# RoPE and scores of all position pairs: the first batch of q and k loaded in whole tiles of 2 MB

## The chip, the cores and the metric

The kernel runs on one core of a Trainium2 chip. The time is device time in microseconds (us). For the kernel before, five executions took 799.1 to 802.11 us, with a median of 801.0 us. One execution was profiled; it took 801.33 us.

The core's engines run side by side, each with its own list of instructions in a fixed order, and wait for one another by semaphores: PE (matrix multiply, with PEld for its weight loads), DVE (elementwise), ACT (elementwise and copies), POOL (unused here but for constants), and SP, which in this kernel only issues DMA transfers. DMA transfers move data between the main memory (HBM) and the on-chip memory (SBUF) on 16 DMA engines. SP's transfers go through one queue (q1), ACT's through another (q10).

## The reference

q and k have shape (16, 512, 16, 64): batch, position, head, dimension. Each is rotated position by position with cos and sin of shape (512, 32), and then the scores are taken for each batch and head (the index letters are those of the reference):

```
q1, q2 = q[..., :32], q[..., 32:]
q_rot = concat([q1*cos - q2*sin, q1*sin + q2*cos])     # k_rot likewise
scores = einsum('bshd,bthd->bsht', q_rot, k_rot)        # (16, 512, 16, 512)
```

So s and t are two positions of the same batch and h is a head: for every batch and head, all 512 x 512 position pairs. All is float32. The inputs are 67 MB, the output 268 MB.

## The kernel before

A batch's 512 positions are put on 128 partitions with C = 4 positions each (position = 4p + c), so that a whole batch of q or of k is one tile of 128 partitions x 16 KB: each partition's 16 KB is one contiguous run in HBM. Work goes in *steps* n = 0 to 63, four (c = 0 to 3) for each batch. For a step, DVE rotates 128 positions of all heads in place (`rope`: a product with `ss_t`, which holds sin and -sin, a product with cos, and an add; lines 146, 147, 151), PE transposes the result 128 columns at a time (`transposed`, L173) and ACT or DVE copies it back over its source (L174). `scores` (L181) then multiplies two heads at a time, and ACT copies the result from PSUM into a staging buffer (L188). When a step's 16 heads are done, SP stores 4 MB (L79).

The order of everything is written out by hand (`manual_schedule`): the order of the statements is the order on each engine. A transfer that stands behind another on SP is issued behind it.

Batch 0 is done differently, so that output can begin before all of it is rotated. Its q and k lie in `early`, the last third of the staging area, which is not yet needed for output. They are worked on in *units*: G = 4 heads of all four positions c, since the scores of a head need all 512 positions of k. `load_units` loads k and q of heads 0 to 3 (512 KB each, in runs of 4 x 64 x 4 B = 1 KB), then k and q of heads 4 to 15 (1.5 MB each, in runs of 3 KB). Behind these SP requests k and q of batch 1, 2 MB each in runs of 16 KB (`load`, L104).

The tables cos and sin, 64 KB each, are requested on ACT's queue (L203) ahead of all. ACT makes `ss_t` from sin (L210, L211). Then come the rope and the transposes of k unit 0 and q unit 0, and a loop over eight pairs of heads (`p` in `range(HP)`, L218): two pairs for each c, with a store of 1 MB (four heads, L222) after every second pair. In this loop stand the rope and transposes of k units 1 and 2 (`run(dve[:2])`, `tr_act`), k of batch 2 is requested after the second store (p = 3) and q of batch 2 after the fourth (p = 7), both L224. The next loop (`for i in range(C)`, L232) does heads 4 to 15 of batch 0, four stages of 3 MB (L251), while DVE goes on to batch 1; its first stage goes to a part of the staging area of its own, its second to where the first three 1 MB stores are read from, so that ACT waits there until these have landed. k of batch 3 is requested after the second of these stores and q of batch 3 after the fourth.

From step 4 on (L258) the staging area is used as three buffers of 4 MB, and k and q have three tiles each. ACT waits before it writes into a buffer whose store has not landed.

Of the kernel before, what the change touches and what calls it, by code (L numbers as in the profile page):

```python
# [10 lines left out]
def kernel(  # L11
# [8 lines left out]
    nc = tc.nc  # L20
    fp32 = mybir.dt.float32
# [3 lines left out]
    B, S, H, D = q.shape  # L25
    HD = D // 2
    P = 128
    C = S // P
    HP = H // 2
    NST = B * C  # L30
    G = H // C
# [3 lines left out]
    in_pool = ctx.enter_context(tc.tile_pool(name="in", bufs=2))  # L35
# [6 lines left out]
    dram = {  # L42
        "q": q.rearrange("b (p c) h d -> b p c h d", c=C),
        "k": k.rearrange("b (p c) h d -> b p c h d", c=C),
    }
# [20 lines left out]
    early = stage_t[:, 3 * RW :]  # L66
# [3 lines left out]
    def stage(i):  # L70
        at = (3 * RW, 0, W)[(i - C) % 3]
        return stage_t[:, at : at + W].rearrange("p (h t) -> p h t", t=S)

    def store(i, st):
        b, c = divmod(i, C)
        if i == NST - 1:
            last(o_v[b, :, c], st)
        else:
            nc.sync.dma_start(o_v[b, :, c], st)  # L79


    units = {}
    used = [0]

    def load_units(which, head, heads):
        n = C * heads * D
        t = early[:, used[0] : used[0] + n].rearrange("p (c e) -> p c e", c=C)
        used[0] += n
        src = dram[which][0, :, :, head : head + heads, :]
        nc.sync.dma_start(t.rearrange("p c (h d) -> p c h d", d=D), src)  # L90
        if which == "q" and head > 0:
            units["r"] = t
        for h in range(0, heads, G):
            units[which, (head + h) // G] = t[:, :, D * h : D * (h + G)]

    tiles = {}
    def load(which, b):

        if b >= B:
            return  # L100
        t = in_pool.tile([P, C, H * D], fp32, tag=which + "_in", bufs=3, name=which + "_sb")
        for c in range(C):
            tiles[which, C * b + c] = t, c
        nc.sync.dma_start(t.rearrange("p c (h d) -> p c h d", h=H), dram[which][b])  # L104

    def slot(which, n):
        if which == "r":
            return units["r"][:, n]
        t, c = tiles[which, n]
        return t[:, c]  # L110

    def unit(which, n):
        return which != "r" and n < C

    def rope(which, n):

        part = part_pool.tile([P, H * D], fp32, tag="part", name="part")
        if unit(which, n):  # L120
            x = units[which, n]
            cs = cos_t.unsqueeze(2).to_broadcast((P, C, 2 * G, HD))
            ss = ss_v.unsqueeze(2).to_broadcast((P, C, G, D))
            sv, k1, k2 = "p c (g j) -> p c g j", {"j": HD}, {"j": D}
            pv = part.rearrange("p (c g j) -> p c g j", c=C, j=D)
            x5 = x.rearrange("p c (h x j) -> p c h x j", x=2, j=HD)
            p5 = part.rearrange("p (c h x j) -> p c h x j", c=C, x=2, j=HD)
            adds = [(x5[:, :, :, y], p5[:, :, :, 1 - y]) for y in range(2)]
        else:
            x = slot(which, n)  # L130
            heads = x.shape[-1] // D
            part = part[:, : heads * D]
            c = n % C
            cs = cos_t[:, c].unsqueeze(1).to_broadcast((P, 2 * heads, HD))
            ss = ss_v[:, c].unsqueeze(1).to_broadcast((P, heads, D))
            sv, k1, k2 = "p (g j) -> p g j", {"j": HD}, {"j": D}
            pv = part.rearrange(sv, **k2)
            x4 = x.rearrange("p (h x j) -> p h x j", x=2, j=HD)
            swapped = bass.AP(
                part.tensor, part.offset + HD, [part.ap[0], (D, heads), (-HD, 2), (1, HD)]  # L140
            )
            adds = [(x4, swapped)]
        xs, xc = x.rearrange(sv, **k2), x.rearrange(sv, **k1)

        def products():
            nc.vector.tensor_tensor(pv, xs, ss, op=mult)  # L146
            nc.vector.tensor_tensor(xc, xc, cs, op=mult)  # L147

        def sums():
            for y, z in adds:  # L150
                nc.vector.tensor_tensor(y, y, z, op=add)  # L151

        return [products, sums]

    def block(which, n, hp):


        if n == 0:
            return units[which, hp // 2][:, :, P * (hp % 2) : P * (hp % 2 + 1)]
        return tiles[which, C * n][0][:, :, P * hp : P * (hp + 1)]  # L160

    def transposed(which, n, g, copy):
# [30 lines left out]
    def tr_act(which, n):  # L193
        for g in range(2):
            transposed(which, n, g, nc.scalar.copy)

    def run(ops):
        for op in ops:
            op()

    with tc.manual_schedule():
        for t, src in ((cos_t, cos), (sin_t, sin)):
            nc.scalar.dma_start(t, src.rearrange("(p c) j -> p c j", c=C))  # L203
        for head, heads in ((0, G), (G, H - G)):
            load_units("k", head, heads)
            load_units("q", head, heads)
        load("k", 1)
        load("q", 1)
        make_identity(nc, ident)
        nc.scalar.copy(out=ss_t[:, :, 0, :], in_=sin_t)  # L210
        nc.scalar.mul(ss_t[:, :, 1, :], sin_t, -1.0)  # L211
        for which in ("k", "q"):
            run(rope(which, 0))
            tr_act(which, 0)


        dve = rope("k", 1) + rope("k", 2) + rope("k", 3) + rope("r", 0)
        for p in range(HP):  # L218
            c, hp = divmod(p, 2)
            scores(block("q", 0, hp)[:, c], block("k", 0, hp), st_all[:, 2 * p : 2 * p + 2])  # L220
            if hp == 1:
                nc.sync.dma_start(o_v[0, :, c, :G], st_all[:, G * c : G * (c + 1)])  # L222
            if p in (3, 7):
                load("kq"[p // 4], 2)  # L224
            if p in (2, 6):
                run(dve[:2])
                dve = dve[2:]
                tr_act("k", 1 + p // 4)
        run(dve)
        tr_act("k", 3)  # L230
        tr_act("r", 0)
        for i in range(C):  # L232
            st = st_rest[i]
            if i < C - 1:
                dve = rope("k", C + i) + rope("r", i + 1)
                nxt = [("k", C + i), ("r", i + 1)]
            else:
                dve = rope("q", C) + rope("k", C + i) + rope("q", C + 1) + rope("k", 2 * C)
                nxt = [("q", C), ("k", C + i)]
            for p in range(R // 2):  # L240
                scores(
                    slot("r", i)[:, P * p : P * (p + 1)],
                    block("k", 0, G // 2 + p),
                    st[:, 2 * p : 2 * p + 2],
                )
                if p in (2, 4):
                    run(dve[:2])
                    dve = dve[2:]
                    tr_act(*nxt.pop(0))
            run(dve)  # L250
            nc.sync.dma_start(o_v[0, :, i, G:], st)  # L251
            if i == 1:
                load("k", 3)
            elif i == C - 1:
                load("q", 3)


        for i in range(C, NST):  # L258
            b, c = divmod(i, C)
            tr = {}  # L260
            if i + 1 < NST:
                tr[1], tr[3] = ("q", i + 1, 0), ("q", i + 1, 1)
            if i + C < NST:
                tr[5], tr[6] = ("k", i + C, 0), ("k", i + C, 1)
            dve = []
            if i + 2 < NST:
                dve += rope("q", i + 2)
            if i + 1 + C < NST:
                dve += rope("k", i + 1 + C)
            st = stage(i)  # L270
            for p in range(HP):
                scores(slot("q", i)[:, P * p : P * (p + 1)], block("k", b, p), st[:, 2 * p : 2 * p + 2])
                if p not in tr:
                    continue
                if tr[p][0] == "q":
                    run(dve[:1])
                    dve = dve[1:]
                    transposed(*tr[p], nc.vector.tensor_copy)
                else:
                    transposed(*tr[p], nc.scalar.copy)  # L280
            run(dve)
            store(i, st)
            if c == 1 and b > 1:
                load("q", b + 2)
            elif c == C - 1:
                load("k", b + 3)
# [30 lines left out]
```

## Time and profile before

| | |
|---|---|
| median of five executions | 801.0 us (799.1 to 802.11) |
| profiled execution | 801.33 us, span 799.4 us |
| busy: PE, DVE, ACT | 689.8 us (86%), 541.7 us (68%), 564.5 us (71%) |
| DMA queue of SP (q1) | 16368 packets, 335.55 MB, 98.5% of the 16 engines' span |
| HBM | 67.24 MB read, 268.44 MB written, 420 GB/s over the span |
| packets under 2 KB, under 8 KB | 2960, 4112 (of 16694) |
| DVE's first product | at 5.93 us |
| first store issued | at 20.19 us |
| last store issued | at 778.12 us |

The span is the time from the program's first instruction to its last; the rest of the execution's time lies around it. Times in the trace count from the span's start. A DMA's "time to landing" runs from its issue to the moment its last part has arrived. The share of the DMA engines can be a little over 1 in a short stretch, where a packet's time includes some overlap with its neighbour.

### The profile page before, as it was taken

The numbers are of one execution on the slowest core, as the hardware profiler recorded it, in microseconds if no ns is written. First come the engines' busy times: TensorE is split into PE (matmuls) and PEld (weight loads), VectorE is DVE, ScalarE is ACT, GpSimd is POOL, SyncE is SP. The second block draws the span as 40 slices with busy tenths as digits, with TensorE's granted clock in tenths as the row PEclk, the third lists the DMA queues.
The fourth block names the chain that finished last, engine by engine and source line by source line (L and its number), as shares of the span: only waits on it lengthen the run. The fifth ranks groups of instructions, "written<-read, shape, count | busy, mean of one in ns | idle before, by whom it ended". The sixth has DMA issues, their size and how long they took to land.

```text
span 799.4 us, 8186 instructions
## 1 busy us (share of the span) xinstructions
PE 689.8 (86%) x3072; PEld 298.9 (37%) x3072; DVE 541.7 (68%) x510; ACT 564.5 (71%) x655; POOL 0.7 (0%) x6
## 2 busy tenths in 40 slices
PE   4999899988979889898978989789897899979960
PEld 2454343433334333343333434334343333334420
DVE  6999778766677666775857757668576686757300
ACT  2998686866768667776757767577775767758870
POOL 0000000000000000000000000000000000000000
PEclk9999999998999989998989989899898998989995
DMA  9999999999999999999999999999999999999996
GB/s 350 425 429 430 435 432 430 424 432 426 431 432 430 432 423 430 432 440 421 441 422 433 431 436 425 429 431 428 432 400 439 426 431 432 402 409 401 421 419 249
DMA packets 16694, 336.19 MB, mean 421 GB/s; under 512 B 1680, under 2 KB 2960, under 8 KB 4112
## 3 DMA queue, kind: packets, MB, share of 16 engines
q1 hardware_dynamic: 16368, 335.55, 98.5%
q8 instruction: 24, 0.39, 0.2%
q10 hardware_dynamic: 288, 0.13, 0.1%
q14 instruction: 14, 0.11, 0.0%
HBM read 67.24 MB, written 268.44 MB: 420 GB/s over the span
## 4 chain that ended last, share of the span: by engine, by line
DMA 49%; PE 36%; DVE 7%; ACT 4%; issue 1%; ACTq 0%; DVEq 0%
DMA out_dram<-st 48%; PE ps L181 27%; PE bank L173 9%; ACT st L188 4%; DVE part L146 2%; DVE st L147 1%; DVE st L151 1%; DVE k_sb L147 1%; DVE k_sb L151 1%; DMA st<-in_k_dram 1%; DVE q_sb L147 0%; DVE q_sb L151 0%; ACTq L312 0%; ACTq L188 0%; DVE q_sb L174 0%
## 5 line engine op out<-in xcount | busy, mean ns | idle before, releaser
L188 ACT COPY st<-ps 128x1024 f32<-128x1024 f32 x512 | 495.2, 1019 | 200.5 <-DMA out_dram<-st 107.7
L181 PE MATMUL ps<-k_sb,q_sb 64*128 64x512 f32 x1920 | 514.7, 653 | 73.2 <-ACT st L188 73.1
L181 PEld LDWEIGHTS ps<-k_sb,q_sb 64*128 64x128 f32 x1920 | 172.4, 197 | 251.4 <-issue 138.5
L174 DVE COPY q_sb<-bank 128x512 f32<-128x512 f32 x118 | 81.6, 691 | 205.7 <-PE bank L173 205.7
L173 PEld LDWEIGHTS bank<-ident,q_sb 128*128 128x128 f32 x480 | 56.0, 153 | 102.5 <-issue 100.9
L173 PE MATMUL bank<-ident,q_sb 128*128 128x128 f32 x480 | 87.4, 310 | 0.0
L173 PEld LDWEIGHTS bank<-ident,k_sb 128*128 128x128 f32 x480 | 50.5, 141 | 91.2 <-DVE k_sb L147 37.7
L173 PE MATMUL bank<-ident,k_sb 128*128 128x128 f32 x480 | 78.0, 286 | 0.1
L147 DVE TENSOR_TENSOR k_sb<-k_sb,cos_t 128x1024 f32<-128x1024 f32 x60 | 73.5, 1225 | 2.9
L147 DVE TENSOR_TENSOR q_sb<-q_sb,cos_t 128x1024 f32<-128x1024 f32 x60 | 73.5, 1225 | 2.1
L151 DVE TENSOR_TENSOR k_sb<-k_sb,part 128x1024 f32<-128x1024 f32 x60 | 73.5, 1225 | 2.1
L146 DVE TENSOR_TENSOR part<-q_sb,ss_t 128x1024 f32<-128x1024 f32 x60 | 73.5, 1225 | 2.0
L146 DVE TENSOR_TENSOR part<-k_sb,ss_t 128x1024 f32<-128x1024 f32 x60 | 73.0, 1216 | 0.2
L151 DVE TENSOR_TENSOR q_sb<-q_sb,part 128x1024 f32<-128x1024 f32 x60 | 73.0, 1216 | 0.1
L174 ACT COPY k_sb<-bank 128x512 f32<-128x512 f32 x120 | 71.4, 599 | 0.0
L181 PE MATMUL ps<-st 64*128 64x512 f32 x128 | 32.5, 639 | 0.4 <-ACT st L174 0.4
L173 PE MATMUL bank<-ident,st 128*128 128x128 f32 x64 | 10.7, 317 | 12.3 <-DVE st L151 9.8
L181 PEld LDWEIGHTS ps<-st 64*128 64x128 f32 x128 | 11.7, 197 | 13.5 <-issue 8.2
L174 ACT COPY st<-bank 128x512 f32<-128x512 f32 (+1 forms) x18 | 9.1, 557 | 8.3 <-PE bank L173 8.3
L173 PEld LDWEIGHTS bank<-ident,st 128*128 128x128 f32 x64 | 8.2, 161 | 17.5 <-issue 12.1
L146 DVE TENSOR_TENSOR part<-st,ss_t 128x1024 f32<-128x1024 f32 (+1 forms) x9 | 10.0, 1106 | 6.2 <-ACT ss_t L211 5.9
L151 DVE TENSOR_TENSOR st<-st,part 128x512 f32<-128x512 f32 (+1 forms) x14 | 10.3, 765 | 0.3
(11 smaller groups left out, 13.8 us busy)
## 6 DMA issues: line engine op xcount, KB each, us to landing
out_dram<-st SPq DMA_DIRECT2D x59, 4096.0 KB, 25.4
k_sb<-in_k_dram SPq DMA_DIRECT2D x15, 2048.0 KB, 28.2
q_sb<-in_q_dram SPq DMA_DIRECT2D x15, 2048.0 KB, 27.7
out_dram<-st SPq DMA_DIRECT2D x4, 3072.0 KB, 13.9
out_dram<-st SPq DMA_DIRECT2D x4, 1024.0 KB, 12.0
out_dram<-st SPq DMA_DIRECT2D x1, 3584.0 KB, 21.5
st<-in_k_dram SPq DMA_DIRECT2D x1, 1536.0 KB, 9.0
st<-in_q_dram SPq DMA_DIRECT2D x1, 1536.0 KB, 12.2
```

Source lines behind the costliest of these rows:

```text
L146: nc.vector.tensor_tensor(pv, xs, ss, op=mult)
L147: nc.vector.tensor_tensor(xc, xc, cs, op=mult)
L151: nc.vector.tensor_tensor(y, y, z, op=add)
L173: nc.tensor.transpose(bank[:, y, :], x[:, y], ident)
L174: copy(out=x, in_=bank[:, :m])
L181: nc.tensor.matmul(out=ps[:, r, :].rearrange("s (c t) -> s c t", c=C), lhsT=lhs[64 * r : 64 * r + 64], rhs=rhs[64 * r : 64 * r + 64], star ...
L188: nc.scalar.copy(out=so.rearrange("s r (t c) -> s r t c", c=C), in_=ps.rearrange("s r (c t) -> s r t c", c=C),)
```

## The change

q and k of batch 0 are each loaded by one transfer of 2 MB, in runs of 16 KB, to the same place as before (`early`). The order of requests on SP becomes k 0, q 0, k 1, q 1, k 2, all ahead of the first store; q of batch 2 is requested after the second store (p = 3) instead of the fourth. `load_units` goes, and the units are now views into the whole tiles: unit n is columns 4 x 64 x n to 4 x 64 x (n + 1) of each position c. Which instructions PE, DVE, ACT and POOL execute, and their order, is as before, except that the rows of a unit now lie 4 KB apart in SBUF instead of 1 or 3 KB.

```diff
-    units = {}
-    used = [0]
-
-    def load_units(which, head, heads):
-        n = C * heads * D
-        t = early[:, used[0] : used[0] + n].rearrange("p (c e) -> p c e", c=C)
-        used[0] += n
-        src = dram[which][0, :, :, head : head + heads, :]
-        nc.sync.dma_start(t.rearrange("p c (h d) -> p c h d", d=D), src)
-        if which == "q" and head > 0:
-            units["r"] = t
-        for h in range(0, heads, G):
-            units[which, (head + h) // G] = t[:, :, D * h : D * (h + G)]
+    first = {}
+    for x, which in enumerate("kq"):
+        t = early[:, C * H * D * x : C * H * D * (x + 1)]
+        first[which] = t.rearrange("p (c e) -> p c e", c=C)
...
-        t = in_pool.tile([P, C, H * D], fp32, tag=which + "_in", bufs=3, name=which + "_sb")
+        if b == 0:
+            t = first[which]
+        else:
+            t = in_pool.tile([P, C, H * D], fp32, tag=which + "_in", bufs=3, name=which + "_sb")
...
-            return units["r"][:, n]
+            return first["q"][:, n, G * D :]
...
-            x = units[which, n]
+            x = first[which][:, :, G * D * n : G * D * (n + 1)]
...
-            return units[which, hp // 2][:, :, P * (hp % 2) : P * (hp % 2 + 1)]
+            return first[which][:, :, P * hp : P * (hp + 1)]
...
-        for head, heads in ((0, G), (G, H - G)):
-            load_units("k", head, heads)
-            load_units("q", head, heads)
-        load("k", 1)
-        load("q", 1)
+        for which, b in (("k", 0), ("q", 0), ("k", 1), ("q", 1), ("k", 2)):
+            load(which, b)
...
-            if p in (3, 7):
-                load("kq"[p // 4], 2)
+            if p == 3:
+                load("q", 2)
```

## The prediction

> **What bounds the kernel now.** I read the page from the engines down to the DMA queues. No compute engine fills the span (PE 86%, ACT 71%, DVE 68%), but the 16 DMA engines do, in every slice but the last.
>
> ```profile
> span 799.4 us, 8186 instructions
> ...
> DMA  9999999999999999999999999999999999999996
> GB/s 350 425 429 430 435 432 430 424 432 426 431 432 430 432 423 430 432 440 421 441 422 433 431 436 425 429 431 428 432 400 439 426 431 432 402 409 401 421 419 249
> ...
> q1 hardware_dynamic: 16368, 335.55, 98.5%
> ```
>
> The reader is to see one queue, that of SP (q1), carry 335.55 MB at about 430 GB/s, which makes 780 us of a span of 799.4. The waits from 60 us on say the same from the other side: ACT, which fills the staging buffers, waits for stores to land.
>
> ```profile
> ACT st L188 <- DMA out_dram<-st: 107.7, 32, 6.0
> ```
>
> So the end is the time of the first byte, plus the bytes at their rate, plus whatever time the queue stands empty. A change of the loads can act on these three alone. The start, cut into stretches (the columns are span of time, its length, busy time of PE, PEld, DVE, ACT and POOL, granted clock, DMA share, GB/s):
>
> ```profile
> 1.00:2.00 1.00, 0.00 (x0) 0.00 (x0) 0.00 (x0) 0.37 (x1) 0.29 (x1) 1.00 0.13 38
> 2.00:3.00 1.00, 0.00 (x0) 0.00 (x0) 0.00 (x0) 0.91 (x1) 0.00 (x0) 1.00 0.74 203
> 3.00:5.00 2.00, 0.00 (x0) 0.00 (x0) 0.00 (x0) 0.00 (x0) 0.00 (x0) 1.00 0.85 251
> 5.00:7.20 2.20, 0.00 (x0) 0.00 (x0) 1.24 (x2) 0.51 (x2) 0.00 (x0) 1.00 1.05 380
> 7.20:13.00 5.80, 1.94 (x8) 1.57 (x8) 5.66 (x7) 1.17 (x2) 0.00 (x0) 1.00 1.02 406
> ...
> 25.00:65.00 40.00, 39.02 (x204) 19.23 (x204) 38.79 (x36) 38.21 (x52) 0.00 (x0) 1.00 1.01 431
> ```
>
> Up to 7.2 us, while the two 512 KB pieces with their 1 KB runs move, the queue does 203 to 380 GB/s, first with idle engines and then at full share; during the 3 KB runs 406; from the 16 KB runs on about 430. Last, the issues of the start with their times to landing (from two stretches of the DMA view), and SP's own issues:
>
> ```profile
> k_sb<-in_k_dram SPq DMA_DIRECT2D x1, 2048.0 KB, 16.5
> ...
> st<-in_q_dram SPq DMA_DIRECT2D x1, 1536.0 KB, 12.2
> st<-in_q_dram SPq DMA_DIRECT2D x1, 512.0 KB, 5.8
> ...
> q_sb<-in_q_dram SPq DMA_DIRECT2D x1, 2048.0 KB, 20.3
> ```
>
> ```profile
> 4.49 0.46 SPq L104 DMA_DIRECT2D q_sb<-in_q_dram  x1
> 20.19 3.28 SPq L222 DMA_DIRECT2D out_dram<-st  x2
> ...
> 28.17 0.42 SPq L104 DMA_DIRECT2D q_sb<-in_q_dram  x1
> 38.37 7.83 SPq L251 DMA_DIRECT2D out_dram<-st  x2
> ```
>
> The last load of the start is issued at 4.49 and lands at 4.49 + 20.3 = 24.8; the one before it at 3.44 + 16.5 = 19.9. So 2 MB of 16 KB runs take 4.9 us. The first store is issued at 20.2, before the loads have run out.
>
> **The change, part by part.**
>
> *Run length of the first batch.* Load data starts at about 2.2 (in the second before it only the tables move), 1.4 us after SP's first issue at 0.73. Four loads of 2 MB at 4.9 make 2.2 + 19.6 = 21.8, plus 0.3 for the two tables of 64 KB between them (128 KB at 430 GB/s): 22.1, or 22.3 if the engines start staggered. Against 24.8 that is a saving of 2.5 to 2.7 us. By bytes it comes out lower: from 2 to 5 us 0.705 MB moved where 430 GB/s would have moved 1.29 (1.35 us lost), from 5 to 7.2 0.25 us, from 7.2 to 15 0.4 us, together 2.0. The landing decides when a buffer is free, so I take 2.5 and keep 2.0 and 2.7 as ends. SP issues two DMAs fewer, some 0.6 us each, at a time when nothing waits behind them.
>
> The Trainium skill, "DMA: Bandwidth & Descriptors", Specifications, gives 512 B as the size from which transfers run at line rate. By that rule runs of 1 KB lose nothing, the saving would be about 0 and the time that of before, 801. The row of 5 to 7.2 us (share 1.05, yet 380 GB/s) speaks against the rule, and I go by the row.
>
> *Later start of the compute.* Now the k piece lands at 0.73 + 5.10 = 5.83 (first step of the chain), and DVE starts at 5.93, when ACT has made ss_t from the sin table. After the change the whole of k lands at about 2.2 + 4.9 + 0.3 = 7.4 and q at 12.3. DVE's rope of k (9.78 - 5.93 = 3.85 us) ends at 11.3 and then waits for q: 12.4 instead of 9.78, a delay of 2.6 us. This is not made up soon: DVE is busy 59.38 us of the 61.07 between 5.93 and 67, in one order, and the scores and so the stores hang on it. The sin table can make the delay longer. It goes on ACT's queue, issued at 1.15, landing after 4.2 us, beside 1 KB packets; in the new kernel beside 16 KB packets of 4.9 / 8 = 0.61 us each (2 MB are 128 runs over 16 engines). Its 128 rows are 8 for each engine. If nothing changes it lands at 5.4; if each row lets one 16 KB packet pass, it takes 8 x 0.61 = 4.9 us from its first row, which comes at some 2.6: 7.5; at the worst 4.9 on top of today's 5.4, 10.3. ACT then takes 0.5 us for ss_t, and DVE starts between 7.5 and 10.8, which makes the delay 2.6 to 4.9. I take 2.9, nearest to the row of one-for-one with a little stagger.
>
> "DMA: Bandwidth & Descriptors", Queues, rings and completion order, says that an engine changes between queues at packets of 9 to 17 descriptors. By it the sin rows would wait once for 9 to 17 of the 0.61 us, an estimate of 5.5 to 10.4 us, and DVE would start at 8.6 to 13.5; no row here shows it.
>
> *k of batch 2 before the first store, q of batch 2 after the second instead of the fourth.* No byte is added. SP issues them without a wait (0.4 to 1.0 us each; the second stands where the first stood, ahead of the third store, whose wait for ACT covers it). The stores of the first stage land up to 4.9 us further back; ACT needs their room in the second of the following stages, at about 38.4 + 2.9 = 41.3, when the third has landed at 22.3 + 4.9 + 2 x 2.45 + 4.9 + 2.45 = 39.5. It costs nothing, with 1.8 us to spare.
>
> *Does the queue run dry?* The spare time is smallest at the stores of line 251. The first is issued at 38.37, when the queue is filled to the landing of the q load, 28.17 + 16.8 = 45.0; the second at 38.37 + 7.83 - 0.33 = 45.87, when it is filled to 38.37 + 13.9 = 52.3. That is 6.4 us, less the 1.4 from issue to first byte: 5.0 us of spare. All requests up to there are the same in sum as before, since the early loads only come sooner. So the queue ends these bytes 2.5 sooner, and the stores come 2.9 later: 5.4 against 5.0, a gap of 0.4 us. The net gain is the smaller of the saving (2.5) and 5.0 less the delay (2.1 at a delay of 2.9, 2.4 at 2.6). At 53.3 and later a load stands in front as well (the queue is then more than 10 us ahead), so no more is lost.
>
> *Sum.* The profiled execution took 801.33 for its span of 799.4, 1.9 us around it, and stands 0.3 above the median of 801.0. Less 2.1 to 2.5, I take 2.3: 799.0 for that execution, and 798.7 against the median.
>
> **The rivals.**
>
> *The delay eats the saving.* If sin lands one packet per row after today's time, the delay is 3.4 to 5.0 and the net gain 1.6 to 0: 799.4 to 801.0. For it: the sin table already takes 4.2 us for 64 KB today. Against it: with a quarter as many pieces in SP's first requests, its rows should start sooner.
>
> *The sin table comes last (the other side).* If each of its 8 rows lets two or three 16 KB packets pass, it lands at 2.6 + 9.8 = 12.4 to 2.6 + 14.7 = 17.3. DVE, whose first product reads ss_t, starts at 13.0 to 17.9, 7.1 to 12.0 late, and the spare of 5.0 is gone: the queue is empty for the rest, 2.1 to 7.0 us slower, 803.1 to 808.0. It decides (slower by over 0.3%) from a landing at about 12.7. For it: the wait for sin ends last already today. Against it: the 1 KB packets of today don't push sin back so far.
>
> *The start is worth more.* If the slow start of the first pieces also staggers the engines (the last store's engines end over 10 us apart, slice 40 at 249 GB/s), an even start could be worth 4 us: 797.0. Nothing in the early rows speaks for it; most of the unevenness comes later.
>
> **How the numbers follow.** About 0.3% (2.4 us) is what a measurement of this kernel can tell from no change. The forecast's case has 0.58; its own range is 797.8 to 799.5, its bound for "faster" at 798.6, and with the executions of before spread over 3 us I give 0.36 to beyond and 0.22 to within. The eaten saving has 0.18, all within. The late sin has 0.19, slower. The better start has 0.05, faster. That makes 0.41 faster, 0.40 same, 0.19 slower. For 8 in 10 the range goes from 797.2, which leaves out most of the better start, to 803.2, which takes in the eaten saving and the lower end of the late sin.
>
> **What would show it.** Right: the stretch from 3 to 20 us at about 430 GB/s throughout; q of batch 1 landing near 22.2; DVE's first product at 7.5 to 8.5 and its rope of q at 12.4 to 12.9; SP's first store near 23; DMA share near 1 from 40 to 55 us, with a dip of under half a microsecond; ACT's waits for stores unchanged after 90 us. Wrong: DVE's first product after 11 us with a long wait for ss_t (sin late); a share well under 1 between 40 and 50 us (spare overrated); landing of q of batch 1 after 23.5 (the saving is smaller than read).

## The result and the profile after

The changed kernel is slower: 805.68 us (median of 41 executions) against 800.93 us for the kernel before (78), a ratio of 1.0051 with a 95% interval of 1.0039 to 1.0062, or 4.1 us (3.1 to 5.0). The ratio is that of the means, 805.93 and 801.85 us; the medians lie 4.75 us apart, since the slower executions of the kernel before reach further above its median (up to 808.75 us). The forecast was 2.3 us faster. The profiled execution took 803.77 us (span 801.7), one of the fastest of the 41, and 2.4 us more than the profiled one of the kernel before. From the page:

```profile
span 801.7 us, 8181 instructions
...
DMA  8999999999999999999999999999999999999996
GB/s 369 376 398 393 431 441 425 428 424 431 424 439 424 438 423 437 423 436 424 430 428 432 434 423 435 425 434 431 437 423 437 423 432 419 428 422 385 437 423 253
...
q1 hardware_dynamic: 14544, 335.55, 98.4%
```

The bound has not moved: the same bytes, on the same queue, at about 430 GB/s from the fifth slice on. What was lost was lost in slices 2 to 4 (20 to 80 us): 376, 398 and 393 GB/s, where the kernel before had 425, 429 and 430. In the kernel before the queue had a slow first slice and then stayed near 430 until slice 29; here it starts a little better and then sags.

The reason stands in the first 20 us. These are the issues of the start with their time to landing (two stretches of the DMA view), and then what DVE waited for up to 20 us:

```profile
st<-in_k_dram SPq DMA_DIRECT2D x1, 2048.0 KB, 8.4
cos_t<-in_cos_dram ACTq DMA_DIRECT2D x1, 64.0 KB, 6.5
...
st<-in_q_dram SPq DMA_DIRECT2D x1, 2048.0 KB, 13.0
...
sin_t<-in_sin_dram ACTq DMA_DIRECT2D x1, 64.0 KB, 11.2
...
q_sb<-in_q_dram SPq DMA_DIRECT2D x1, 2048.0 KB, 21.8
```

```profile
DVE part L139 <- ACT ss_t L201: 12.9, 1, 12.9
```

The sin table, 64 KB, takes 11.2 us (4.2 before) and lands at 1.16 + 11.2 = 12.4 us. DVE, whose first product reads ss_t, starts at 12.93 instead of 5.93. All of k had landed at 0.74 + 8.4 = 9.1, so 3.8 us of this wait are for the table alone. SP's issues show the delay arriving at the stores:

```profile
26.61 3.23 SPq L212 DMA_DIRECT2D out_dram<-st  x2
29.89 0.46 SPq L97 DMA_DIRECT2D q_sb<-in_q_dram  x1
31.33 3.16 SPq L212 DMA_DIRECT2D out_dram<-st  x2
45.30 7.83 SPq L241 DMA_DIRECT2D out_dram<-st  x2
```

The first store comes at 26.61 instead of 20.19, the first 3 MB store at 45.30 instead of 38.37: 6.9 us late.

How the table is held up can be counted. In the stretch from 4 to 7 us:

```profile
q1 hardware_dynamic: 79, 1.29, 100.6%
q10 hardware_dynamic: 78, 0.03, 3.8%
```

79 packets of SP's queue and 78 of ACT's: one for one (28 and 28, 22 and 21, 29 and 29 in the three single microseconds). SP's are 16 KB (1.29 MB / 79), ACT's are table rows of 512 B. cos and sin have 128 rows each, that is 16 for each of the 16 engines, and each row lets one packet of 0.61 us pass: with 0.03 us for the row itself (both from the shares above), 16 x 0.64 = 10.2 us from about 2 us on. In the kernel before, the rows stood beside packets of 1 KB, and cos was all but through at 2.2 us (139 of ACT's 288 packets), when these began.

Where did the queue lose its bytes? The same stretches of both kernels, first before, then after (the last two columns are the DMA share and GB/s):

```profile
0.00:25.00 25.00, 13.25 (x56) 7.63 (x57) 18.59 (x20) 10.96 (x16) 0.70 (x6) 1.00 0.92 363
...
25.00:75.00 50.00, 48.96 (x252) 23.51 (x252) 48.66 (x45) 46.67 (x62) 0.00 (x0) 1.00 1.01 430
...
0.00:95.00 95.00, 80.72 (x392) 39.04 (x392) 85.40 (x81) 71.81 (x94) 0.70 (x6) 1.00 0.99 413
```

```profile
0.00:25.00 25.00, 6.25 (x24) 4.32 (x26) 11.76 (x13) 4.47 (x8) 0.70 (x6) 1.00 0.91 380
...
25.00:75.00 50.00, 48.27 (x252) 23.39 (x248) 48.62 (x46) 47.07 (x63) 0.00 (x0) 1.00 0.98 382
...
45.00:60.00 15.00, 15.00 (x80) 7.17 (x78) 14.55 (x14) 14.94 (x21) 0.00 (x0) 1.00 0.94 400
60.00:75.00 15.00, 14.88 (x78) 6.91 (x74) 14.66 (x14) 13.92 (x18) 0.00 (x0) 1.00 1.02 384
0.00:95.00 95.00, 74.50 (x368) 36.57 (x368) 79.83 (x76) 68.57 (x90) 0.70 (x6) 1.00 0.97 393
```

At 25 us the changed kernel is ahead by 17 x 25 = 0.42 MB, 1.0 us of the queue. At 95 us it is behind by 20 x 95 = 1.9 MB, 4.4 us. From 25 to 75 us (430 and 382 GB/s) it loses 2.4 MB, 5.6 us; the share of busy engines falls only from 1.01 to 0.98, which is 1.5 us. The other 4 us are engines that count as busy and move less, most plainly from 60 to 75: share 1.02, 384 GB/s. The loss is complete at 95 us: from there to 400 us both kernels move 430 GB/s. That 4.4 us is close to the 4.1 of the ratio is partly chance, for these two executions end only 2.3 us apart: from 400 to 600 us the changed kernel moves 430 GB/s and the kernel before 428, from 600 to 780 us 423 and 420. Why the kernel before is slower there was not tried.

### The profile page after: what moved, and what is told of

Its sections match the earlier page's. It is cut to its first block, busy times and chain, and to the rows that moved or that the text cites. A ratio compares the mean times of both kernels' runs of the same rounds, so it can differ in the third digit from the quotient of the medians.

```text
span 801.7 us, 8181 instructions
## 1 busy us (share of the span) xinstructions
PE 687.3 (86%) x3072; PEld 298.9 (37%) x3072; DVE 541.7 (68%) x510; ACT 564.4 (70%) x655; POOL 0.7 (0%) x6
## 4 chain that ended last, share of the span: by engine, by line
DMA 49%; PE 34%; DVE 7%; ACT 4%; issue 1%; ACTq 0%
DMA out_dram<-st 49%; PE ps L174 26%; PE bank L166 8%; ACT st L181 4%; DVE part L139 2%; DVE st L140 1%; DVE st L144 1%; DVE k_sb L144 1%; DVE k_sb L140 1%; DVE q_sb L140 0%; DVE q_sb L144 0%; ACTq L302 0%; ACTq L181 0%; DVE q_sb L167 0%
## 5 line engine op out<-in xcount | busy, mean ns | idle before, releaser
L166 PEld LDWEIGHTS bank<-ident,k_sb 128*128 128x128 f32 x480 | 50.5, 141 | 91.0 <-issue 35.5
L139 DVE TENSOR_TENSOR part<-st,ss_t 128x1024 f32<-128x1024 f32 (+1 forms) x9 | 10.0, 1107 | 13.2 <-ACT ss_t L201 12.9
```

The source lines that it names most:

```text
L166: nc.tensor.transpose(bank[:, y, :], x[:, y], ident)
```

## The experiments

The theory was: the tables are held up by 16 KB packets, everything starts late, and the queue has less to do than it can. The rivals: the new order of requests costs the time (stores land later); the 16 KB runs or the new layout do. The time and the profile of a run are read apart, since a profile shows one execution, and executions of one kernel lie some 3 us apart or more. In microseconds the ratios below are taken against 800.9.

**Tables first.** The changed kernel with

```diff
-            nc.scalar.dma_start(t, src.rearrange("(p c) j -> p c j", c=C))
+            nc.sync.dma_start(t, src.rearrange("(p c) j -> p c j", c=C))
```

> The changed kernel with one edit: SP requests cos and sin, ahead of k of batch 0, instead of ACT on its own queue. The theory (the tables alternate row for row with 16 KB packets, sin lands at 12.4 instead of 5.3 us, everything starts 7.0 us late and the store queue's spare time of 5.0 us is used up): sin lands before 4 us, DVE's first product starts at about 8 us, the first store is issued near 23 us, and the time is 1.5 to 2.5 us below the kernel before (ratio 0.997 to 0.998). The rival that the new order of requests (k 2 ahead of the first store) costs the time, and the rival that the layout or the 16 KB runs do: the tables' queue makes no difference, ratio 1.004 to 1.006 as for the changed kernel.

Measured: 1.0013 (0.9989 to 1.0037), +1.0 us. Three of the four microseconds are gone with this one line. (The profiled execution, 806.13 us, is the slowest of its twelve, whose median is 802.02; what is read here is its start.) sin lands at 1.20 + 2.0 = 3.2, and DVE now waits for k:

```profile
9.59 1.23 DVE L139 TENSOR_TENSOR part<-st,ss_t 128x1024 f32<-128x1024 f32 x1 [9.59 <-DMA st<-in_k_dram]
```

That refutes both rivals as the main cause, since the order, the 16 KB runs and the layout are still in this kernel; the product takes 1.23 us here and with the old layout (1.22 and 1.23), so that the layout costs it nothing. It also refutes the forecast's sum: k lands at 9.5, where the sum had 7.4, so that the first store is issued at 25.14 and not near 23, and no gain shows against the kernel before.

**The order alone.** The kernel before with the changed kernel's requests:

```diff
         load("q", 1)
+        load("k", 2)
...
-            if p in (3, 7):
-                load("kq"[p // 4], 2)
+            if p == 3:
+                load("q", 2)
```

> The kernel before (pieces of 512 KB and 1.5 MB) with the order of requests of the changed kernel alone: k of batch 2 ahead of the first store, q of batch 2 after the second. The theory: tables and first pieces land as before, DVE starts at 5.9 us, nothing is late, ratio 0.999 to 1.001. The rival of the order: the stores of the first stage land 4.9 us later and this costs it, ratio 1.004 to 1.006.

Measured: 1.0007 (0.9983 to 1.0031). DVE starts at 5.81. The order costs nothing that can be measured: the interval reaches 2.5 us, but up to 95 us the queue moves 413 GB/s, exactly as in the kernel before.

**The run length alone.** The changed kernel with k and q of batch 2 requested where they were:

```diff
-        for which, b in (("k", 0), ("q", 0), ("k", 1), ("q", 1), ("k", 2)):
+        for which, b in (("k", 0), ("q", 0), ("k", 1), ("q", 1)):
...
-            if p == 3:
-                load("q", 2)
+            if p in (3, 7):
+                load("kq"[p // 4], 2)
```

> The changed kernel with k and q of batch 2 requested at their old places (after the second and the fourth store). The theory: sin is late as in the changed kernel and the first store comes at 26.6 us, but now only 8 MB stand ahead of it, which land at 24.0; with 1.4 us from issue to first byte the queue is empty for 4.0 to 4.5 us in sum, less 0.8 us for the earlier landing of the first loads: 3.5 us above the kernel before (1.0045) by this sum, against 1.9 by the same sum for the changed kernel (measured 1.0051), so 1 to 2 us slower than the changed kernel. The rival of the order: the cause is gone, ratio about 1.000 or below.

Measured: 1.0074 (1.0051 to 1.0097), +5.9 us. The rival of the order falls here too: with the old order the time does not come back. Whether it is worse than the changed kernel, as expected, the overlapping intervals leave open, and sin also landed later in this profile (14.0 us, DVE at 14.56). Only four loads stand ahead of a store that comes at 27.98, and now the queue is plainly empty; from 25 to 45 us the profile has a share of 0.80:

```profile
25.00:45.00 20.00, 16.95 (x24) 1.00 0.80 294
```

(This view shows ACT's busy time alone ahead of clock, share and GB/s.) The share alone makes 0.2 x 20 = 4 us.

**The tables' place by itself.** The kernel before with the one-line edit of the first experiment.

> The kernel before with cos and sin requested by SP ahead of the first pieces: the price of this edit by itself. The theory: sin lands before 4 us instead of 5.3, the first k piece at 5.8 to 6.4, so that DVE starts within 0.5 us of its old place; ratio 0.999 to 1.001. If a large part of the gain of the changed kernel with tables first came from the tables' place alone, this kernel would show it: 0.998.

Measured: 1.0011 (0.9980 to 1.0041); DVE starts at 5.77. Within this interval the tables' place is worth nothing where the pieces are of 1 KB runs.

**Shorter runs beside the tables.** The changed kernel with its first two loads cut by positions, `w` = 2 (runs of 8 KB) or 1 (4 KB):

```diff
-        nc.sync.dma_start(t.rearrange("p c (h d) -> p c h d", h=H), dram[which][b])
+        w = 2 if b == 0 else C
+        for c in range(0, C, w):
+            v = t[:, c : c + w].rearrange("p c (h d) -> p c h d", h=H)
+            nc.sync.dma_start(v, dram[which][b, :, c : c + w])
```

> The changed kernel with k and q of batch 0 in two transfers of 1 MB each, in runs of 8 KB (two positions at a time), tables on ACT's queue as they were. The theory of row-for-row alternation: cos and sin have 16 rows on each DMA engine, each lets one packet pass, now 0.31 us long: about 5.4 us from the first row, so sin lands at 7.5 to 8.5 us (12.4 with 16 KB packets); the wait is then for k (about 9 us) and no longer for sin; delay of the first store 4 to 5 us, time 0 to 1.5 us above the kernel before (1.000 to 1.002). The rival (sin waits behind all loads requested before it, or for bytes whatever their packets): sin stays at 12 us and the ratio at 1.004 to 1.006.

> The same with four transfers of 512 KB each, in runs of 4 KB. Alternation: 16 rows at 0.16 + 0.03 us make 3.0 us: sin lands at 5 to 6 us. If the slow start that the profile with the tables first shows (k landing at 9.5 us, where 7.4 was expected) comes from the long first packets, k lands earlier here, at 7.5 to 8.5 us, and q at 12.5 to 13.5; delay of the first store 2.7 to 3.7 us, inside the spare time; time -1.5 to +0.5 us against the kernel before (0.998 to 1.0005). If the slow start is the same for every run length, k lands at 9.5, q at 14.4, and the ratio is 1.001 to 1.002 as with the tables first.

Measured: 0.9986 (0.9966 to 1.0007) with 8 KB, 1.0015 (0.9994 to 1.0036) with 4 KB. sin's time to landing, 11.2 us with 16 KB packets, is 5.6 with 8 KB; it lands at 6.8 us, a little before the 7.5 to 8.5 expected. The exchange was not one for one throughout: from 5.4 to 6.1 us 121 packets of ACT's queue stand against 45 of SP's. With 4 KB sin lands at 6.9 us and not at 5 to 6: below 8 KB something else than the packets passed sets it. In both kernels DVE then waits for k; with 8 KB:

```profile
8.95 1.23 DVE L142 TENSOR_TENSOR part<-st,ss_t 128x1024 f32<-128x1024 f32 x1 [8.95 <-DMA st<-in_k_dram]
```

With 4 KB it starts at 9.42, hardly earlier than with the tables first and 16 KB (9.59). So the long first packets are not the main reason that 2 MB land so late; the expectation of 7.5 to 8.5 is a miss.

**Lateness by itself.** The kernel before, its loads untouched, with three or six extra products on DVE ahead of the first rope (they write scratch that is overwritten later):

```diff
+        idle = part_pool.tile([P, H * D], fp32, tag="part", name="part")
+        idle = idle.rearrange("p (c g j) -> p c g j", c=C, j=D)
+        twice = ss_v.unsqueeze(2).to_broadcast((P, C, G, D))
+        for _ in range(3):
+            nc.vector.tensor_tensor(idle, twice, twice, op=mult)
         for which in ("k", "q"):
             run(rope(which, 0))
```

> The kernel before with three extra products on DVE ahead of the first rope (ss_t times itself into the scratch tile, 1.25 us each; results are as before): everything starts 3.8 us late and no transfer is changed. The theory of spare time (5.0 us, or 4.2 if the first byte takes longer after an empty queue): inside it, ratio 0.999 to 1.001. The rival that any late start is paid in full: 3.8 us, 1.0047.

> The same with six extra products: 7.5 us late, a little over the 7.0 of the changed kernel. The theory: 7.5 less 4.2 to 5.0 is 2.5 to 3.3 us, ratio 1.003 to 1.004, with DMA share under 1 at about 27 and between 44 and 56 us. The rival that a late start is paid in full: 7.5 us, 1.0094. The rival that lateness is not the cause at all: 1.000.

Measured: 1.0027 (1.0006 to 1.0048), +2.2 us for 3.8 us late, and 1.0079 (1.0049 to 1.0109), +6.3 us for 7.5. Lateness alone costs time. The expectations used the spare time of the new order for a kernel with the old one; there it is smaller, 2.7 us (the second store, issued at 20.19 + 3.28 - 0.33 = 23.13 when the queue is filled to 27.3, that is 24.8 and 1 MB more, less 1.4). By that 1.1 and 4.8 us follow, inside both intervals and below both values. But the rival that a late start is paid in full, 1.0047 and 1.0094, lies inside both intervals as well, and these two runs do not rule it out.

**Lateness with the new order.** The same extra products in the kernel of the second experiment (order alone, old pieces, tables as before):

> The order of requests of the changed kernel, the old pieces, and three extra products on DVE ahead of the first rope (3.8 us late). The spare time of 5.0 us that the prediction worked out belongs to this order, not to the old one (with the old order the second store, with only 8.4 MB and one store ahead of it, leaves 27.3 - 23.1 - 1.4 = 2.7 us). If 5.0 is right: 1.000. If the queue loses more than the sum says, as in the run with three extra products and the old order (2.2 us where 1.1 follows from 2.7): 1.001 to 1.002.

> The same with six extra products: 7.5 us late, with no other trace of the changed kernel's loads or tables. If the delay is the whole cause, this shows what the changed kernel loses: by a spare of 5.0 us 2.5 us (1.003); the changed kernel's 4.1 us at 7.0 us late and 0.8 us saved mean a spare of 2.1 us, and then 5.4 us here (1.0067). If it stays at 1.003, the changed kernel has a second cause of about 2 us that is not the delay.

Measured: 1.0002 (0.9984 to 1.0021) and 1.0052 (1.0034 to 1.0070), +4.2 us. This is the decisive pair. Both intervals leave out payment in full (1.0047 and 1.0094). The second kernel has none of the changed kernel's loads and no late table; it is merely late, by 13.63 - 5.93 = 7.7 us at DVE:

```profile
13.63 1.23 DVE L146 TENSOR_TENSOR part<-st,ss_t 128x1024 f32<-128x1024 f32 x1
```

It loses what the changed kernel loses, and in the same way: a slow stretch from 60 to 75 us, and 388 GB/s up to 95 us

```profile
60.00:75.00 15.00, 14.91 (x78) 6.93 (x74) 14.66 (x13) 13.93 (x17) 0.00 (x0) 1.00 0.99 374
0.00:95.00 95.00, 74.47 (x364) 36.53 (x364) 86.49 (x82) 67.98 (x89) 0.70 (x6) 1.00 0.97 388
```

So the late start is the whole cause, within the intervals of some 1.5 us (the table in the next section puts it more sharply), and the slow stretch of the queue belongs to lateness and not to 16 KB loads at the start or to the layout. (The expectation's remark that the changed kernel's numbers mean a spare of 2.1 us subtracted the saving of 0.8 once too often: once the queue starves, an earlier landing is already in the spare. 7.0 - 4.1 is 2.9.)

**The changed kernel again.**

> The changed kernel once more, beside the others on the same chip: 1.004 to 1.006, sin landing at 12.4 us. Its second profile shows whether the slow load of k of batch 3 (62.5 to 70.4 us, 7.9 us for 2 MB) and of q of batch 2 (7.0 us) belongs to this kernel: at the same two loads again, or elsewhere.

Measured: 1.0066 (1.0043 to 1.0089). This time sin took 12.9 us and landed at 14.1, not at 12.4: of ACT's rows none moved before 2 us, where the first profile had 32 packets. The exchange was again one for one (79 and 79 from 4 to 7 us). DVE started at 14.62, and the first 3 MB store came at 47.39, 9.0 us late. The profiled execution, 808.84 us, is the slowest of nine (median 806.21). From 60 to 75 us the queue moved 374 GB/s at a share of 1.00, so the slow stretch is there again.

**The 8 KB variant again.**

> The variant with runs of 8 KB again (0.9986 with an interval of 0.9966 to 1.0007 the first time): whether it beats the kernel before. By the sums: first loads landing 1.2 us earlier, first store 4.4 us late, which is inside a spare of 5.0 and outside one of 2.1; so 0.9985 by the first and 1.001 by the second.

Measured: 1.0001 (0.9980 to 1.0023). It takes back what the changed kernel loses, but does not beat the kernel before.

## Why the prediction was wrong

**The bound and the frame were right.** The end is the queue's: at 95 us the changed kernel is 1.9 MB behind, 4.4 us, and by the ratio it ends 4.1 us later. The order of requests costs nothing that shows (1.0007), and a delay is paid only beyond a spare time. All three signs that the prediction gave for being wrong came: DVE's first product at 12.93 with a long wait for ss_t, a share under 1 (0.94) from 40 to 50 us, q of batch 1 landing at 24.0. With the measured delay of 7.0 in place of 2.9, its sum gives 5.0 - 7.0: 2.0 us slower. That is two thirds of the way from -2.3 to +4.1; the rest is the spare time.

**The step that failed first: "a delay of 2.6 us ... I take 2.9".** Measured: 7.0 at DVE, 6.9 at the first 3 MB store. Two terms in it were short.
- The sin table. The prediction had the one-for-one exchange between the queues, and counted 8 rows for each engine. But it took for granted that cos would be through before the exchange began, as in the profile before. cos is held up the same way (6.5 us to landing), and sin stands behind it on the same queue: 16 rows, not 8. With that count the prediction's own row gives 2.6 + 16 x 0.61 = 12.4, the measured landing; to the tenth that is luck, since the second profile has 14.1, with the first rows later. One-for-one is also what speaks against the Trainium skill's "DMA: Bandwidth & Descriptors", Queues, rings and completion order, weighed there: with whole packets of 9 to 17 descriptors before each change of queue, the 79 and 78 packets would not match in every microsecond. The range that was worked out from it, DVE at 8.6 to 13.5, takes in the 12.93 of the first profile and not the 14.62 of the second.
- The landing of k. The prediction had 7.4 us: first byte at 2.2, then 2 MB at the steady 4.9. It landed at 9.1, and at 9.5 with the tables out of the way, where DVE started at 9.59. This term alone makes DVE 3.7 us late; the table makes it 7.0.

**The step "so I take 2.5" (the saving) failed for the same reason.** The last load of the start landed at 2.16 + 21.8 = 24.0 instead of 24.8: 0.8 us. The loss at the start was read as the price of 1 KB and 3 KB runs, but a start with long runs has nearly the same loss: with 4, 8 and 16 KB runs the same 8 MB land at 24.2, 23.6 and 24.0 (24.2 with the tables first). The row from 5 to 7.2 us (380 GB/s at full share) remains; it is worth a fraction of a microsecond. To this extent the same page's rule in Specifications, that runs from 512 B go at line rate, was nearer to the result than the prediction's reading, which made 2.5 us of it.

**The step "5.0 us of spare" was too large.** It can be read within one profile: how late the first 3 MB store is issued (against 38.37), and how far the queue is behind the kernel before at 95 us (GB/s up to there against 413, at 430 GB/s).

| kernel | store late, us | GB/s to 95 us | behind, us | late less behind |
|---|---|---|---|---|
| new order, three products | 3.9 | 405 | 1.8 | 2.1 |
| 8 KB, twice | 4.7, 5.0 | 401, 399 | 2.7, 3.1 | 2.0, 1.9 |
| 4 KB | 4.7 | 401 | 2.7 | 2.0 |
| tables first | 5.0 | 399 | 3.1 | 1.9 |
| changed kernel, twice | 6.9, 9.0 | 393, 382 | 4.4, 6.8 | 2.5, 2.2 |
| new order, six products | 7.7 | 388 | 5.5 | 2.2 |
| old order, three products | 3.9 | 398 | 3.3 | 0.6 |
| old order, six products | 7.8 | 379 | 7.5 | 0.3 |
| run length alone (old order) | 8.5 | 379 | 7.5 | 1.0 |

With the new order the spare is 1.9 to 2.5 us in eight profiles, whether the lateness comes from 16 KB loads, from the tables or from added products: about 2.2. So up to 95 us the changed kernel shows no second cause beside its lateness. With the old order the spare is 1 us or less, so that in these profiles the early request of k is worth about a microsecond to a late kernel. By the ratios less is lost than at 95 us (with 8 KB, for one, -1.1 and 0.1 us of 2.7 and 3.1 behind), so that some of it seems to be made up later; how was not tried. Two things are missing in the sum. It counted a landing as the moment up to which the queue is filled, but a landing is that of the last engine: in the trace of the kernel before, the sixteen completions of the first 3 MB store lie between 50.5 and 52.3 us. And it took a nearly empty queue to work at full rate until it is empty; the changed kernel's profile shows 4 us lost by engines that count as busy. That these two make the missing 2.8 us is likely, not shown.

**The rival "the sin table comes last" had the mechanism and the place,** with a chance of 0.19. It wanted two packets to pass for each row; one for each of twice as many rows came to the same landing, 12.4, so that its count was right by luck. Its price there was 7.1 - 5.0 = 2.1 us; with the spare of 2.2 at 95 us it is 4.9, against 4.4 in the profile. "The delay eats the saving" is what remains with the tables first: a delay of 5.0, 1.0 us slower within an interval that takes in no change.

## What to carry to other kernels

In the changed kernel a small transfer on a second queue was served row by row against the first queue's 16 KB packets, so that its time was its rows per engine times the length of such a packet (with 4 KB packets it took longer than that product, 5.7 us to landing). Before making the packets of a first load longer, count all rows of the small tables that the first instruction waits for, and put those tables ahead on the same queue. Where a queue of transfers is the bound, work ahead of the first store is free only up to the spare time, which is worked out at the store where the queue is shortest, and should be taken well below what the sum gives (here 2.2 us, where the sum gave 5.0). A slow first stretch of a queue is not yet the fault of the transfers in it: try another size before booking the whole loss as a saving.

## What the runs showed of the hardware that was not expected

- Two queues exchanged packets one for one although one's were 32 times as long: 79 of 16 KB against 78 of 512 B in 3 us, 79 against 79 in the second profile. Beside 8 KB packets this broke off at the end: 121 rows against 45 packets from 5.4 to 6.1 us, 130 against 43 in that kernel's second profile.
- 2 MB requested first land 7.8 to 8.4 us after their issue, of which some 1.4 pass before the first byte; 2 MB in a full queue take 4.9; runs of 4 and 8 KB hardly shorten the start (DVE at 9.42 and 8.95 us, 9.59 with 16 KB and the tables first). What holds the start back was not settled.
- When the work is late and the queue nearly drained, it moves less from 60 to 75 us at a share of 0.99 to 1.03: 384 and 374 GB/s in the two profiles of the changed kernel, 374 with six extra products, 393 with the tables first, 395 to 398 with 8 and 4 KB, 411 with three extra products, where the kernel before moves 436. With the old order it did not in that stretch, late or not (428 with the run length alone, 423 with three extra products), but with three extra products it did earlier: 379 GB/s at a share of 0.99 from 25 to 45 us, where the kernel before moves 433. Why busy engines move less there is open; nothing was tried on it.
